# The order of a small product, two state loads and a norm broadcast in a one-core hybrid decoder step

## The chip, the cores and the metric

The kernel runs on one core of a Trainium2 chip. The metric is device microseconds (us) of one execution. An engine takes its instructions in the order in which they stand in its own queue: TensorE (PE, matrix products, with its weight loads shown apart as PEld), VectorE (DVE), ScalarE (ACT), GpSimd (POOL), and SyncE (SP), which here only issues transfers (DMA). Engines meet through semaphores, so an instruction that waits holds back all that stand behind it on its engine.

## What is computed

One layer of a hybrid decoder, for a prompt of 1024 tokens and for 8 sample sequences of 4 tokens (1056 columns in all, the last 32 being the samples). All data are float32; large products are made of three products of rounded halves, so that each counts three times on PE. Cut to what matters here:

```python
proj = rmsnorm(x, norm1) @ w_in                # -> z | x,B,C | dt | q | k | v
xbc  = silu(causal_conv4(x,B,C))
# state-space mixer, 8 heads in 2 groups, chunks of 128 tokens:
cb     = C_chunk @ B_chunk.T                   # one 128x128 product per chunk and group
y_diag = (cb * decay) @ (x * dt)
y_off  = C_chunk @ state * exp(acum)           # the state that came in
state  = state * chunk_decay + B_chunk.T @ (x * tail)
y = rmsnorm((y + x*d_skip) * silu(z))
# beside it windowed attention over q, k, v -> y_att
x  = x + concat(y, y_att) @ w_out
u  = causal_conv3(rmsnorm(x, norm2) @ w_up)
x  = x + (silu(gate) * val) @ w_down
```

For the sample sequences `state` is read from an input (8 states for each group of heads, 1 MB per group here), for the prompt it starts at zero.

## The kernel before

Activations lie with features on the 128 partitions and tokens along the columns. The program has these stretches, by the times of the profile: the input projection and the attention, to about 265 us; the state-space mixer with the projection for z, the last projections for x,B,C and the first output pieces between its steps, to about 390 us; the remaining output pieces, to 465 us; the up projection with its convolution, to 930 us (it is done in halves of 528 columns, tp = 0 and 1, and by a seven-product scheme on 2x2 blocks, whose block sums, `T1` to `T4` and the like, are made by VectorE); and the down projection, to the end.

The order is set in two steps. The string `PLAN` lists the steps of the mixer stretch: `u` a state unit (group, chunk; chunk 8 is the samples), `x` a projection with its convolution, `z` a gate block, `n` a gate norm, `a` and `s` the splitting of attention and mixer output into rounded halves, `o` an output piece (row block m, column quarter q). Then a list scheduler with a timeline of its own (`schedule_with_timeline_sim=True`) reorders the instructions of every engine, and so an edit in one function can move instructions of many others. Tiles come from pools with a fixed number of buffers; a tile of a full pool waits until the last reader of an older one is done.

What the change and the prediction touch:

- `ssd_unit(g, t, ...)` is one state unit. It transposes x (two blocks) and B into the PSUM tile `px` (L611), ACT copies them to `xt` (L614), POOL multiplies by dt and by the tail into `xw` and `xd` (L618, L619). The product of B and C, `pcb`, goes to the last 128 columns of the same `px` (L638), and VectorE masks it into `cb` (L640), which multiplies the decay `M` (tile `ab`, L646). Then come the products into `yy` (L653, L655) and the new state into `st` (L660).
- Its sample branch (t = 8) multiplies `xw` (L674), stores `bt` and `xd` to `smps` (L678, L679), and loads the 8 incoming states in four transfers of 256 KB into the two buffers of `h0` (L682), each followed by two products into `yy` (L685); `ys` (L687, L689) adds up, `yt` (L692) transposes back.
- The pool with the tag `y` has eight buffers; `fm` (the eight blocks of x, B and C), `yt` (attention output read back, L751) and `acc` (the residual read from `in_xT`, L774) take turns in them.
- `half_rstd(tp)` sums squares by products with ones (L852), takes the reciprocal root on VectorE (L134 to L140), transposes the six columns back to rows by PE (L859) and copies them (L861). `half_prep(tp)` calls it, scales the residual (L871) and makes the operands of the up projection (L883, L884, L888). It is called for tp = 0 between two output pieces of the first row block and for tp = 1 after the first up product (L1068).
- L147 is the inner product of all dense work (`dense`), L990 that of the up projection, L998 and L1012 add two of its products, L935 and L936 split its weights.

Of the kernel before, what the change touches and what calls it, by code (L numbers as in the profile page):

```python
# [46 lines left out]
def kernel(ctx, tc, xT, wxbc, wkv, wq, wz, wout, wup, wdn, cols, rows, cst, idm,  # L47
# [29 lines left out]
    def b3(ap, *shape):  # L77
        return ap.broadcast_to(list(shape))
# [519 lines left out]
    def ssd_unit(g, t, p, carry, te):  # L598
# [5 lines left out]
        hs = slice(4 * g, 4 * g + 4)  # L604
        px = psd.tile([128, 512], F32, tag="px", name="px", bufs=2)
        if smp:
            f4 = p.tile([128, 512], F32, tag="Cs", name="f4", bufs=2)[:, 0:384].rearrange("p (i c t) -> p i c t", i=3, c=4)
            for i, f in enumerate((x0, x1, Bm)):
                pool.tensor_copy(out=f4[:, i], in_=b3(f[:, tok].unsqueeze(1), 128, 4, NS))
        for i, f in enumerate((x0, x1, Bm)):  # L610
            pe.transpose(out=px[:, i * 128:(i + 1) * 128],  # L611
                         in_=f4[:, i].rearrange("p c t -> p (c t)") if smp else f[:, tok], identity=ident)
# [21 lines left out]
            act.activation(out=M[:, h], in_=M[:, h], func=AF.Relu, scale=-1.0,  # L634
                           bias=acum[:m, t, 4 * g + h:4 * g + h + 1])
        act.activation(out=M, in_=M, func=AF.Exp, scale=-1.0)
        pcb = px[:m, 384:384 + m]
        pe.matmul(out=pcb, lhsT=Bm[:, tok], rhs=Cm[:, tok], start=True, stop=True)  # L638
        cb = p.tile([128, 128], F32, tag="cb", name="cb")[:m, :m]
        dve.tensor_tensor(out=cb, in0=pcb, in1=(cs[:NS, K_TS:K_TS + NS] if smp else tri), op=ALU.mult)  # L640
        if smp:
# [33 lines left out]
                      rhs=xw[:m, 64 * h:64 * h + 64], start=True, stop=True)  # L675
        cm = p.tile([128, 8, NS], F32, tag="cm", name="cm", bufs=1)
        pool.tensor_tensor(out=cm, in0=b3(Cm[:, NP:T].unsqueeze(1), 128, 8, NS), in1=bmask, op=ALU.mult)
        sp.dma_start(out=smps[g, :, 0:128], in_=bt)  # L678
        sp.dma_start(out=smps[g, :, 128:384], in_=xd)  # L679
        for j in range(4):  # L680
            h0 = p.tile([128, 2, 256], F32, tag="h0", name="h0", bufs=2)
            sp.dma_start(out=h0, in_=h0T[:, g, 2 * j:2 * j + 2])  # L682
            for b in range(2):
                r = slice(32 * (2 * j % 4 + b), 32 * (2 * j % 4 + b) + 32)
                pe.matmul(out=yy[r, 256:512], lhsT=cm[:, 2 * j + b], rhs=h0[:, b], start=j < 2, stop=j >= 2)  # L685
        y = p.tile([128, 256], F32, tag="xd0", name="ys")
        dve.tensor_tensor(out=h4(y), in0=h4(yy[:, 256:512]),  # L687
                          in1=b3(te[:, 8 + 4 * g:12 + 4 * g].unsqueeze(2), 128, 4, 64), op=ALU.mult)
# [160 lines left out]
    def half_rstd(tp):  # L849
        ps = bank()  # L850
        for j in range(6):
            pe.matmul(out=ps[:88, j:j + 1], lhsT=ssum[tp][:, 88 * j:88 * j + 88], rhs=ones[:, 0:1], start=True, stop=True)  # L852
        v = pt_.tile([128, 2, 6], F32, tag="v2", name="v2")
        dve.tensor_scalar(out=v[:88, 0], in0=ps[:88, 0:6], scalar1=1.0 / D, scalar2=EPS, op0=ALU.mult, op1=ALU.add)
        rsqrt(pt_, v[:88, 1], v[:88, 0], 88, 6)
        for q in range(2):
            ps = bank()
            for j in range(3):
                pe.transpose(out=ps[:, 88 * j:88 * j + 88], in_=b3(v[:88, 1, 3 * q + j:3 * q + j + 1], 88, 128),  # L859
                             identity=ident[:88, :88])  # L860
            act.activation(out=ssum[tp][:, q * QC:q * QC + QC], in_=ps[:, :QC], func=AF.Copy)  # L861
        return ssum[tp]

    X2 = [{}, {}]

    def half_prep(tp):

        rb = half_rstd(tp)
        for m in (4, 5, 6, 7, 0, 1, 2, 3):
            h = half(m, tp)  # L870
            dve.scalar_tensor_tensor(out=h, in0=h, scalar=col(C_N2 + m), in1=rb, op0=ALU.mult, op1=ALU.mult)  # L871
# [73 lines left out]
    for i, m in enumerate((4, 5, 6, 7, 0, 1, 2, 3)):  # L945
        if i >= 4:
            w[m] = None
        for q in (2, 3):
            out_piece(m, q)
            if i == 0 and q == 2:  # L950
                half_prep(0)
        half_done(m, 1, i == 0)
    up_load(0)
    for j in range(7):
# [93 lines left out]
    for n, (cp, groups) in enumerate(SETS):  # L1048
        for g in groups:
# [15 lines left out]
                conv(cp, 0)  # L1065
            last = (n, *g), done
            if g == (0, 0):
                half_prep(1)  # L1068
    product(*last[0], 6)
    conv(last[0][1], 1)  # L1070
    sp.dma_start(out=fco, in_=fcot)
# [188 lines left out]
```

## Time and profile before

| | before |
|---|---|
| runs, us | 1192.59, 1192.26, 1187.1 |
| median, us | 1192.26 |
| the profiled execution, us | 1191.26 |
| its span, first to last instruction, us | 1189.5 |
| mean granted TensorE clock | 0.99 |
| PE busy | 1149.4 (97%) |
| VectorE busy | 906.0 (76%) |
| ScalarE busy | 513.0 (43%) |
| GpSimd busy | 134.8 (11%) |
| moved by DMA | 122.52 MB, mean 103 GB/s |

A row of the window table gives, for a stretch, its length and then the busy time and the number of instructions of PE, PEld, DVE, ACT and POOL, the granted clock of TensorE (1.00 is full speed), the busy share of the DMA engines and the rate. A row of the timeline gives start, length, engine, line, operation and tile, with "x4" where four like ones are merged, and in brackets how long the engine had been idle before and who released it. A row of the chain of waits gives start and length of a piece of the chain that ended last. The profiled execution is 1.76 us longer than its span.

### The profile page before, as it was taken

Reading aid. Unit: us, or ns where it says so; the run is one execution under the profiler, and the core shown is the slowest. Engines: PE = TensorE matmul, PEld = TensorE weight load, DVE = VectorE, ACT = ScalarE, POOL = GpSimd, SP = SyncE. Lnnn points to the kernel's source line nnn. Section 1 sums busy time; section 2 is a strip of 40 time slices with the busy share of each in tenths; the row PEclk is TensorE's granted clock in tenths of the full one; section 3 lists DMA queues with packets and bytes.
Section 4 is the critical chain, followed back from the end, with each engine's and each line's share of the span. In section 5 each row is a group of like instructions: output and inputs, shape, how many; then the busy total and the mean of one; then the engine's idle time right before and its main releaser. Section 6 shows DMA issues by size and latency. Waiting matters only on the chain.

```text
span 1189.5 us, 22050 instructions
## 1 busy us (share of the span) xinstructions
PE 1149.4 (97%) x8614; PEld 1106.5 (93%) x8614; DVE 906.0 (76%) x1886; ACT 513.0 (43%) x1048; POOL 134.8 (11%) x300
## 2 busy tenths in 40 slices
PE   8899989999979999899999999999999999999998
PEld 7899878888957999789999999999999999999998
DVE  7678868666888578998777777787777877677764
ACT  7435553446774334555455454545454421112110
POOL 0000001022253000011011010101010011001000
PEclk9999989998999999899999999999999999999999
DMA  8111102113465523122222222222222944224203
GB/s 295 63 60 62 33 19 75 48 50 111 131 221 160 173 73 131 36 81 98 74 72 90 73 90 73 90 73 81 81 71 75 380 149 160 97 91 133 92 9 147
DMA packets 52360, 122.52 MB, mean 103 GB/s; under 512 B 9232, under 2 KB 19984, under 8 KB 52240
## 3 DMA queue, kind: packets, MB, share of 16 engines
q1 hardware_dynamic: 52256, 121.12, 29.8%
q8 instruction: 67, 1.10, 0.4%
q14 instruction: 37, 0.30, 0.1%
HBM read 94.86 MB, written 27.26 MB: 103 GB/s over the span
## 4 chain that ended last, share of the span: by engine, by line
PE 89%; DVE 7%; DMA 2%; ACT 1%; issue 1%; SPq 0%; POOL 0%; DVEq 0%; ACTq 0%
PE ps L147 40%; PE ps L990 35%; PE ps L199 7%; PE sc L503 1%; PE ps L525 1%; DVE x2l L884 1%; DVE au L936 1%; DVE c L1032 1%; PE two L147 1%; DMA raw<-in_wup 1%; PE ps L517 1%; PE yy L653 1%; PE st L660 1%; PE ps L339 0%; PE px L611 0%
## 5 line engine op out<-in xcount | busy, mean ns | idle before, releaser
L990 PE MATMUL ps<-x2h,au 128*128 128x264 f32 x2464 | 456.1, 286 | 8.5 <-DVE au L936 2.8
L990 PEld LDWEIGHTS ps<-x2h,au 128*128 128x128 f32 x2464 | 385.0, 189 | 10.6 <-DVE au L936 3.5
L990 PE MATMUL ps<-x2l,au 128*128 128x264 f32 x1232 | 349.4, 285 | 0.1
L990 PEld LDWEIGHTS ps<-x2l,au 128*128 128x128 f32 x1232 | 232.8, 189 | 0.3 <-DVE x2l L884 0.3
L1105 DVE TENSOR_TENSOR acc<-acc,ps 128x352 f32<-128x352 f32 x264 | 131.5, 517 | 66.0 <-PE ps L147 65.5
L147 PE MATMUL ps<-xh,uh 128*128 128x264 f32 (+3 forms) x528 | 163.3, 315 | 8.9 <-ACT xh L182 5.9
L147 PE MATMUL ps<-gh,ul 128*128 128x352 f32 x528 | 170.1, 322 | 0.0
L147 PE MATMUL ps<-gl,uh 128*128 128x352 f32 x528 | 170.0, 322 | 0.0
L147 PE MATMUL ps<-gh,uh 128*128 128x352 f32 x528 | 167.8, 322 | 0.0
L147 PE MATMUL ps<-xh,ul 128*128 128x264 f32 (+3 forms) x528 | 163.7, 311 | 0.0
L147 PE MATMUL ps<-xl,uh 128*128 128x264 f32 (+3 forms) x528 | 163.3, 310 | 0.3 <-POOL xl L180 0.3
L116 ACT ACTIVATE uh<-raw 128x1024 fp32r<-128x1024 f32 (+3 forms) x59 | 55.9, 953 | 188.0 <-PE ps L147 166.9
L1032 DVE SCALAR_TENSOR_TENSOR c<-u,colt,c 128x1072 f32<-128x1072 f32 x88 | 116.7, 1329 | 3.6 <-ACT c L1030 3.6
L147 PEld LDWEIGHTS ps<-xh,uh 128*128 128x128 f32 x528 | 99.7, 190 | 13.7 <-ACT xh L182 6.3
L147 PEld LDWEIGHTS ps<-xl,uh 128*128 128x128 f32 x528 | 100.6, 191 | 1.8 <-POOL xl L180 0.9
L147 PEld LDWEIGHTS ps<-xh,ul 128*128 128x128 f32 x528 | 100.6, 190 | 1.0 <-issue 0.3
L936 DVE TENSOR_TENSOR au<-raw,au 128x512 fp32r<-128x512 f32 x115 | 78.8, 690 | 27.3 <-ACT au L935 27.3
L147 PEld LDWEIGHTS ps<-gl,uh 128*128 128x128 f32 x528 | 99.2, 188 | 0.4
L147 PEld LDWEIGHTS ps<-gh,ul 128*128 128x128 f32 x528 | 99.3, 188 | 0.0
L147 PEld LDWEIGHTS ps<-gh,uh 128*128 128x128 f32 x528 | 98.8, 188 | 0.0
L935 ACT ACTIVATE au<-raw 128x512 fp32r<-128x512 f32 x115 | 71.0, 625 | 60.7 <-DVE raw L923 31.5
L119 DVE TENSOR_TENSOR ul<-raw,uh 128x1024 fp32r<-128x1024 f32 (+3 forms) x55 | 60.5, 1105 | 7.0 <-ACT uh L116 6.9
(290 smaller groups left out, 1768.4 us busy)
## 6 DMA issues: line engine op xcount, KB each, us to landing
raw<-in_wup SPq DMA_DIRECT2D x46, 512.0 KB, 3.5
gr<-gd SPq DMA_DIRECT2D x22, 528.0 KB, 5.3
gd<-c SPq DMA_DIRECT2D x22, 512.0 KB, 2.6
raw<-in_wdn SPq DMA_DIRECT2D x22, 512.0 KB, 3.8
raw<-in_wout SPq DMA_DIRECT2D x12, 512.0 KB, 3.4
acc<-in_xT SPq DMA_DIRECT2D x16, 264.0 KB, 5.0
accd<-acc SPq DMA_DIRECT2D x16, 264.0 KB, 2.5
acc<-accd SPq DMA_DIRECT2D x8, 528.0 KB, 8.4
```

The lines of the kernel that those rows point to most:

```text
L116: act.activation(out=hi, in_=raw, func=AF.Copy)
L119: (e or dve).tensor_tensor(out=lo[:, i:i + n], in0=raw[:, i:i + n], in1=hi[:, i:i + n].bitcast(F32), op=ALU.subtract)
L147: pe.matmul(out=ps, lhsT=w(a, k), rhs=x(b, k), start=first and k == ks[0] and i == 0, stop=last and k == ks[-1] and i == 2)
L199: pe.matmul(out=ps[:m, :n], lhsT=x[k][c][:, a:a + m], rhs=w[k // nk][b][:, o:o + n], start=k == 0 and i == 0, stop=k == 7 and i == 2)
L503: pe.matmul(out=sb[:, v, c].rearrange("p i k -> p (i k)"), lhsT=qT[a][r, c], rhs=kT[b][r, o:o + 256], start=i == 0, stop=i == 2)
L517: pe.transpose(out=pt[:, h], in_=P[:, h], identity=ident)
L525: pe.matmul(out=po[64 * v:64 * v + 64, 0:256].rearrange("p (c q) -> p c q", c=2), lhsT=(vall[:, t - i] if i or not t else vdif[:, t - 1])[ ...
L935: act.activation(out=u[:, 0:512], in_=src, func=AF.Copy)
L936: dve.tensor_tensor(out=u[:, 512:1024], in0=src, in1=u[:, 0:512].bitcast(F32), op=ALU.subtract)
L990: pe.matmul(out=ps, lhsT=wgt[:, 512 * a + 128 * k:512 * a + 128 * k + 128], rhs=xx[b][:, k], start=opens and k == 0 and i == 0, stop=k == ...
L1032: dve.scalar_tensor_tensor(out=c[:, 0:n], in0=u[:, j:j + n], scalar=col(C_FW + 3 * m + j), in1=c[:, 0:n], op0=ALU.mult, op1=ALU.add)
L1105: dve.tensor_tensor(out=o, in0=o, in1=ps[:, :PC], op=ALU.add)
```

## The change

Three edits, each of code that is written in another place:

1. In every state unit the product `pcb` of B and C is issued ahead of the three transposes into the same `px`.
2. In the sample units the first two of the four loads of states are written at the unit's beginning; the two stores to `smps` now stand behind all four.
3. `half_prep(0)` is split: the norm sums and the reciprocal root (`half_rstd`) stay after output piece (4, 2), the broadcast and what follows (`half_bcast`) come after piece (4, 3).

```diff
@@ -604,9 +604,17 @@
         px = psd.tile([128, 512], F32, tag="px", name="px", bufs=2)
         if smp:
+
+            h0s = []
+            for j in range(2):
+                h0s.append(p.tile([128, 2, 256], F32, tag="h0", name="h0", bufs=2))
+                sp.dma_start(out=h0s[j], in_=h0T[:, g, 2 * j:2 * j + 2])
             f4 = p.tile([128, 512], F32, tag="Cs", name="f4", bufs=2)[:, 0:384].rearrange("p (i c t) -> p i c t", i=3, c=4)
             for i, f in enumerate((x0, x1, Bm)):
                 pool.tensor_copy(out=f4[:, i], in_=b3(f[:, tok].unsqueeze(1), 128, 4, NS))
+
+        pcb = px[:m, 384:384 + m]
+        pe.matmul(out=pcb, lhsT=Bm[:, tok], rhs=Cm[:, tok], start=True, stop=True)
         for i, f in enumerate((x0, x1, Bm)):
             pe.transpose(out=px[:, i * 128:(i + 1) * 128],
@@ -634,8 +642,6 @@
         act.activation(out=M, in_=M, func=AF.Exp, scale=-1.0)
-        pcb = px[:m, 384:384 + m]
-        pe.matmul(out=pcb, lhsT=Bm[:, tok], rhs=Cm[:, tok], start=True, stop=True)
         cb = p.tile([128, 128], F32, tag="cb", name="cb")[:m, :m]
@@ -675,14 +681,17 @@
-        sp.dma_start(out=smps[g, :, 0:128], in_=bt)
-        sp.dma_start(out=smps[g, :, 128:384], in_=xd)
         for j in range(4):
-            h0 = p.tile([128, 2, 256], F32, tag="h0", name="h0", bufs=2)
-            sp.dma_start(out=h0, in_=h0T[:, g, 2 * j:2 * j + 2])
+            if j < 2:
+                h0 = h0s[j]
+            else:
+                h0 = p.tile([128, 2, 256], F32, tag="h0", name="h0", bufs=2)
+                sp.dma_start(out=h0, in_=h0T[:, g, 2 * j:2 * j + 2])
             for b in range(2):
                 r = slice(32 * (2 * j % 4 + b), 32 * (2 * j % 4 + b) + 32)
                 pe.matmul(out=yy[r, 256:512], lhsT=cm[:, 2 * j + b], rhs=h0[:, b], start=j < 2, stop=j >= 2)
+        sp.dma_start(out=smps[g, :, 0:128], in_=bt)
+        sp.dma_start(out=smps[g, :, 128:384], in_=xd)
@@ -853,6 +862,9 @@
         rsqrt(pt_, v[:88, 1], v[:88, 0], 88, 6)
+        return v
+
+    def half_bcast(tp, v):
         for q in range(2):
             ps = bank()
@@ -863,9 +875,9 @@
-    def half_prep(tp):
-
-        rb = half_rstd(tp)
+    def half_prep(tp, v):
+
+        rb = half_bcast(tp, v)
@@ -948,7 +960,9 @@
             out_piece(m, q)
             if i == 0 and q == 2:
-                half_prep(0)
+                v0 = half_rstd(0)
+            elif i == 0:
+                half_prep(0, v0)
@@ -1065,7 +1079,7 @@
             if g == (0, 0):
-                half_prep(1)
+                half_prep(1, half_rstd(1))
```

What the scheduler made of it shows in the order of the built programs, at three places.

SP's queue around the sample unit of group 0 and after it. `h_3929` and `h_3933` are its first two loads before, `h_3937` and `h_3941` the second two, `h_4631` the first load of group 1; in the change the same are `h_3892`, `h_3894`, `h_3935`, `h_3939` and `h_4594`. Before:

```order
L631 DMA Cs<-ead 128x512
L678 DMA smps<-xt 128x128
L628 DMA ms<-acds 32x128
L679 DMA smps<-xd 128x256
L751 DMA yt<-yatt 128x2x384 x2
L115 DMA raw<-in_wout 128x1024
L628 DMA ab<-acd 128x512 x2
L631 DMA Cs<-ead 128x512
L774 DMA acc<-in_xT 128x528
L628 DMA ab<-acd 128x512
L682 DMA h_3937<-in_h0T 128x512
L682 DMA h_3941<-in_h0T 128x512
```

Now:

```order
L760 DMA yt<-yatt 128x2x384 x2
L636 DMA ms<-acds 32x128
L639 DMA Cs<-ead 128x512
L693 DMA smps<-xt 128x128
L694 DMA smps<-xd 128x256
L636 DMA ab<-acd 128x512 x2
L115 DMA raw<-in_wout 128x1024
L639 DMA Cs<-ead 128x512
L783 DMA acc<-in_xT 128x528 x2
L636 DMA ab<-acd 128x512
L689 DMA h_3935<-in_h0T 128x512
L689 DMA h_3939<-in_h0T 128x512
```

The attention output `yt` is now read ahead of the stores to `smps`, one more residual load stands ahead of the second pair of states, and the first pair stands where it stood: its two rows are far above these, the 62nd and 63rd of SP's queue before and now. The second pair of group 1 stood ahead of the reads of `yt` for the last column block and of eight residual loads; now it stands behind those reads and behind four of the eight loads.

PE at the second pair of states of group 0. Before:

```order
L638 MATMUL px<-fm 128x128 x2
L685 MATMUL yy<-h_3937,cm 32x256 x2
L611 MATMUL px<-idt,fm 128x128 x6
L685 MATMUL yy<-h_3941,cm 32x256 x2
L692 MATMUL yt<-idt,ys 128x128 x2
L660 MATMUL st<-xd,xt 128x256
L638 MATMUL px<-fm 128x128
```

Now:

```order
L147 MATMUL ps<-xh,ul 128x264
L692 MATMUL yy<-h_3935,cm 32x256 x2
L692 MATMUL yy<-h_3939,cm 32x256 x2
L617 MATMUL px<-fm 128x128
L619 MATMUL px<-idt,fm 128x128 x3
L617 MATMUL px<-fm 128x128
L619 MATMUL px<-idt,fm 128x128 x3
L701 MATMUL yt<-idt,ys 128x128 x2
```

The six transposes that stood between the two halves of the second pair are gone from there. Between the first pair and the second stand 17 dense products and two `pcb` before, and 18 dense products, one `pcb` and six transposes now.

VectorE at the preparation of the second half (tp = 1) for the up projection. Before:

```order
L936 TENSOR_TENSOR au<-raw,au 128x512 x2
L871 SCALAR_TENSOR_TENSOR acc<-acc,colt,ssum_5198 128x528 x8
L998 TENSOR_TENSOR u<-s_5934,ps 128x264
L998 TENSOR_TENSOR u<-s_5907,ps 128x264
L884 TENSOR_TENSOR x2l<-acc,x2h 128x528
L936 TENSOR_TENSOR au<-raw,au 128x512
L925 TENSOR_TENSOR t_6025<-raw 128x512
```

Now:

```order
L1012 TENSOR_TENSOR u<-s_5934,ps 128x264
L1012 TENSOR_TENSOR u<-s_5907,ps 128x264
L948 TENSOR_TENSOR au<-raw,au 128x512
L883 SCALAR_TENSOR_TENSOR acc<-acc,colt,ssum_5198 128x528 x8
L937 TENSOR_TENSOR t_6025<-raw 128x512
L896 TENSOR_TENSOR x2l<-acc,x2h 128x528 x5
```

The scaling of the second half stands three instructions later on VectorE. On PE its broadcast stands behind 134 products of the up projection before, and behind 156 now, and the first half's broadcast follows its norm sums by 47 dense products before and by 33 now; after that broadcast come 300 dense products before and 264 now. From the sample unit's first product to the last norm sum of the mixer PE has 153 dense products before and 219 now.

## The prediction

> **What bounds the kernel now.** I read the page's first lines, then the window table, the waits of PE between 255 and 396 us, the timelines of that stretch by engine, and the chain of waits around the norm of the second half.
>
> ```profile
> span 1189.5 us, 22050 instructions
> core 0: us, PE busy (x) PEld busy (x) DVE busy (x) ACT busy (x) POOL busy (x), PEclk, DMA share, GB/s
> 268.00:272.00 4.00, 1.64 (x11) 0.98 (x8) 4.00 (x10) 3.31 (x10) 2.33 (x3) 0.84 0.86 275
> 272.00:278.00 6.00, 6.00 (x19) 5.82 (x20) 4.43 (x9) 5.28 (x15) 1.02 (x2) 0.53 0.39 135
> 330.00:345.00 15.00, 10.44 (x75) 7.49 (x75) 10.45 (x20) 11.92 (x32) 10.48 (x15) 1.00 0.88 301
> 345.00:367.00 22.00, 17.36 (x168) 13.99 (x165) 20.23 (x60) 16.53 (x53) 5.73 (x11) 1.00 0.28 93
> 367.00:390.00 23.00, 21.36 (x167) 18.66 (x165) 18.81 (x63) 7.39 (x17) 10.82 (x14) 1.00 0.59 186
> 390.00:465.00 75.00, 75.00 (x621) 74.79 (x621) 52.97 (x104) 28.76 (x45) 0.40 (x4) 1.00 0.37 126
> 465.00:485.00 20.00, 20.00 (x171) 19.82 (x170) 16.12 (x39) 8.94 (x20) 1.62 (x4) 1.00 0.32 97
> 485.00:515.00 30.00, 24.32 (x163) 22.74 (x162) 28.61 (x50) 16.59 (x31) 0.68 (x4) 0.89 0.17 65
> 515.00:535.00 20.00, 18.22 (x148) 17.80 (x146) 19.66 (x29) 12.37 (x18) 4.10 (x8) 1.00 0.20 63
> 535.00:1189.50 654.50, 649.86 (x4832) 648.97 (x4832) 490.87 (x807) 240.56 (x395) 66.41 (x172) 1.00 0.30 105
> ```
>
> PE bounds all but a few places: from 390 to 485 it never rests, and after 535 it misses 4.6 of 654.5 us. The change takes no instruction away, so it can only win idle PE time. In the mixer stretch that is 4.56 us (330 to 345), 4.64 (to 367) and 1.64 (to 390), 10.8 us in all, and before it the start, where PE is busy for 1.64 of 4 us and then runs 6 us at a clock of 0.53. Elsewhere an edit can lose: in 485 to 535 VectorE is the full engine (28.61 of 30, 19.66 of 20 us) and PE waits for it.
>
> **The product ahead of its transposes.** At the start of the mixer:
>
> ```profile
> 269.64 0.49 PE L638 MATMUL px<-fm 128*128 128x128 f32 x2 [1.09 <-ACT xt L614]
> 271.93 1.22 PE L660 MATMUL st<-xd,xt 128*128 128x256 f32 x2 [0.97 <-POOL xd L619]
> 268.69 0.49 ACT L710 ACTIVATE ps<-gz 128x384 f32<-128x384 f32 x1 [4.48 <-DVE gz L709]
> 269.12 0.47 ACT L614 ACTIVATE xt<-px 128x384 f32<-128x384 f32 x1
> 269.67 1.64 POOL L618 TENSOR_TENSOR xd<-xt,dt 128x256 f32<-128x256 f32 x1 [2.62 <-ACT xt L614]
> 271.27 0.61 POOL L619 TENSOR_TENSOR xd<-xt,tailw 128x256 f32<-128x256 f32 x1
> ```
>
> `pcb` writes the tile that ACT is reading, and so waited 1.09 us for the copy `xt`. Ahead of the transposes it does not. But the next instruction, `st`, waited for POOL until 271.93, and that chain stays: ACT's copy stands behind the gate's L710, which waits for VectorE, then POOL needs 1.64 and 0.61. The wait changes its name, and the dense products behind `st` begin at the same time. Value 0. Bounds: if POOL came earlier by the 1.09, a gain of 1.1; if the now unbroken idle time from about 268.9 to 271.9 prolonged the slow stretch by half of its price (half of (1 - 0.53) x 6.00 = 2.8), a loss of 1.4. From 278 to 330 the units run between dense products; there is nothing to win.
>
> The earlier `pcb` also ends the use of B earlier, and the buffer goes to `yt`:
>
> ```profile
> 327.08 0.88 SPq L751 DMA_DIRECT2D yt<-yatt  x2
> 333.68 3.97 DVE L180 TENSOR_TENSOR xl<-fm,xh 128x384 fp32r<-128x384 f32 x4 [2.41 <-ACT xh L179]
> 268.08 1.40 SPq L682 DMA_DIRECT2D h<-in_h0T  x2
> 334.36 0.90 SPq L682 DMA_DIRECT2D h<-in_h0T  x2
> 339.68 0.63 PE L685 MATMUL yy<-h,cm 128*32 128x256 f32 x4 [2.38 <-DMA h<-in_h0T]
> 340.23 0.88 PE L611 MATMUL px<-idt,fm 128*128 128x128 f32 x6
> 341.04 0.63 PE L685 MATMUL yy<-h,cm 128*32 128x256 f32 x4
> 339.72 0.47 DVE L640 TENSOR_TENSOR cb<-px,cs 128x128 f32<-128x128 f32 x2
> ```
>
> In the new order `yt` stands ahead of the stores, and ACT's splitting, for which VectorE waited 2.41 us, can begin earlier. That alone does not move PE, which then waits for the states.
>
> **The states.** The first pair was issued at 268.08, some 65 us ahead of its products, and stands at the same place now: that part of the edit does nothing. The wait of 2.38 us is for the second pair, issued at 334.36, when the first pair's buffers come free; the edit leaves that as it is. What moves is beside it: between the pairs PE has about four small matmuls more (0.81 us for six, from 340.23 to 341.04, so 0.5 us of cover), and the six transposes between the halves of the second pair are gone, so that `ys` can begin 0.8 us earlier; two `cb` (0.47) now stand between the parts of `ys` on VectorE, which is the full engine from there to 367. One residual load more stands ahead in the queue. Together -1.3 + 0.4 = -0.9, and with `yt` out of the way of the loads I take -1.3. Bounds: 2.38 + 0.8 + the 0.3 that remains of cover = -3.5; if the additional 264 KB at 301 GB/s (0.9 us) land ahead of the states and VectorE sets the end, +1.0.
>
> Group 1's second pair is the part that speaks against the change:
>
> ```profile
> 372.47 0.82 SPq L682 DMA_DIRECT2D h<-in_h0T  x2
> 378.90 3.76 SPq L774 DMA_DIRECT2D acc<-in_xT  x8
> DMA to landing us min/median/max: 3.9/7.0/7.0
> 366.13 1.13 DVE L740 SCALAR_TENSOR_TENSOR fm<-fm,colt,nb 128x384 f32<-128x384 f32 x2
> 378.36 1.49 DVE L180 TENSOR_TENSOR xl<-fm,xh 128x288 fp32r<-128x288 f32 x2 [1.44 <-ACT xh L179]
> 421.49 0.86 PE ps L852 x12
> 422.35 5.83 PE ps L147 x47
> 428.64 36.64 PE ps L147 x300
> 465.28 5.82 PE ps L990 x48
> 473.44 9.39 PE ps L990 x74
> 483.90 3.17 DVE acc L871 x5
> 489.42 0.68 DVE u L998 x2
> L936 DVE TENSOR_TENSOR au<-raw,au 128x512 fp32r<-128x512 f32 x115 | 78.8, 690 | 27.3 <-ACT au L935 27.3
> ```
>
> Before, it was issued at 372.47 and PE did not wait. Now four residual loads stand ahead: 3.76 / 8 = 0.47 us each to issue, 1.9 in all, then 3.9 to 7.0 to land, so 5.8 to 8.9 us. PE's cover between the pairs is 5 + 31 = 36 dense products at 5.83 / 47 = 0.124, or 4.5, and 0.6 for small ones: 5.1. The stall is 0.7 to 3.8, or nothing if the loads go before the buffers come free. I take +1.5, near the low end, since the transfers now stand in a queue that asks for `yt` earlier.
>
> The 66 dense products more in this stretch (219 against 153) are 8.2 us of PE work, but 52 stand ahead of the second sample unit, where PE was idle for 1.64 us in all. I take -1.0 (-1.6 to 0) for that.
>
> **The norm.** Between the first half's sums (421.49) and its broadcast PE did 47 dense products without a pause: there is nothing to win. The new order puts that broadcast 36 products (4.5 us) closer to the up products; VectorE, busy for 52.97 of 75 us until 465, has room. The second half's broadcast stands behind 156 up products in place of 48 + 12 + 74 = 134: 22 at 9.39 / 74 = 0.127, or 2.7 us later, and the scaling (483.90) with it, at the start of the stretch that VectorE fills. VectorE does three instructions more before it, two of 0.34 and one of 0.69: 1.4 us that it need not do after. Value +2.7 - 1.4 = +1.3. Bounds 0 (if the sums wait for VectorE anyway) and +2.7.
>
> **The sum:** 0 - 1.3 + 1.5 - 1.0 + 1.3 = +0.5 us. The profiled execution took 1191.26, which is 1.0 under the median shown, so **1191.8 us**. The bounds add up to -6.2 and +8.9; not all fall on one side, and the forecast's own range is 1187 to 1197.
>
> By the Trainium skill (TensorE: Matmul & The Clock Gate, Part 1), the clock falls to half after an idle window of about 3.4 us and comes back after about 3.4 us of sustained work. The clock of 0.53 after the start and 1.00 around the stall of 2.38 us agree with that in kind, though the start's slow stretch is nearer to 6 us. By it, any stall that this change brings is worth only itself while it stays under 3.4 us; the slow rival below would be 1.7 us of slow clock dearer than its stall, where the row gives 2.8.
>
> **Rivals.**
>
> *Faster: the mixer stretch was held by VectorE and the transfers, and the 66 products fill it.* If the stretch keeps its length while 8.2 us of PE work move into it, the idle 10.8 us shrink by as much, and 1.3 come back in the norm: 1191.26 - 8.2 + 1.3 = 1184.4. For it: VectorE is busy for 20.23 of 22 us in 345 to 367. Against it: in just that window the new order has the same 36 dense products as the old, and the products added stand where PE had little idle time. 0.21.
>
> *Slower: the second pair of group 1 waits behind a residual load whose buffer is not free.* A residual load needs the buffer of a split block. If it waits for the last block, the path is L740 (1.1), ACT's part (about 0.8) and L180 (1.5), 3.4 us after the norm's broadcast, then two issues (0.9) and 7.0 to land: 11.3, against PE's cover from there, 47 dense products (5.8) and 1.1 of small ones. The stall is 4.4, long enough to bring a slow stretch such as that of 272 to 278 (2.8): 7.2 us. The gain of 1.0 is gone, the other terms cancel: 1191.26 + 7.2 = 1198.5. It decides from a stall of about 3.5 us. For it: the queue's order, and the 3.76 us that the eight loads took. Against it: of those eight, issued at 0.47 us each, hardly one waited. 0.14.
>
> *The change does not do what it says.* The scheduler had loaded the states early and put products between sums and broadcast already, and the `pcb` wait was one of several. Then all that is left is a reshuffled order that costs as much as it gains: 1191.3. 0.20.
>
> **How the numbers follow.** The forecast itself has 0.45. It and the third rival are no change within 0.5% (6 us, about what a measurement of this kernel can tell from no change): 0.65. Faster 0.21, slower 0.14. The range 1183.5 to 1199 takes in both other cases' times and leaves out a sum in which nearly all bounds fall on one side.
>
> **What would show it.** Right: no PE wait for `xt` in front of `pcb`, but one at the first `st` until about 272; a wait for the second pair of group 0 of 1 to 2 us; one for group 1's of 0.7 to 2.5; the second half's scaling 2 to 3 us later after the first up product. The forecast is wrong if PE's idle time from 330 to 390 falls below 5 us, or if the wait for group 1's states passes 3.5 us with a clock under 1.00 behind it.

## The result

| | runs | median, us | ratio to before, 95% interval |
|---|---|---|---|
| before | 5 | 1191.3 (1187.1 to 1192.59) | |
| changed | 5 | 1210.58 (1204.56 to 1212.15) | 1.0153 (1.013 to 1.0175) |

The change makes the kernel 1.5% slower. The forecast of 1191.8 us, its range (1183.5 to 1199) and its likeliest cases were wrong.

### The profile page after: what moved, and what is told of

Read it like the earlier page. It is cut to its first block, busy times and chain, and to the rows that moved or that the text cites. A ratio compares the mean times of both kernels' runs of the same rounds, so it can differ in the third digit from the quotient of the medians.

```text
span 1210.3 us, 22105 instructions
## 1 busy us (share of the span) xinstructions
PE 1159.8 (96%) x8614; PEld 1113.0 (92%) x8614; DVE 917.5 (76%) x1886; ACT 517.4 (43%) x1048; POOL 143.0 (12%) x300
## 4 chain that ended last, share of the span: by engine, by line
PE 87%; DVE 6%; DMA 3%; ACT 2%; issue 1%; POOL 0%; SPq 0%; DVEq 0%; ACTq 0%; POOLq 0%
PE ps L147 38%; PE ps L1004 34%; PE ps L199 6%; PE sc L503 1%; PE ps L525 1%; DMA raw<-in_wup 1%; DVE x2l L896 1%; DVE au L948 1%; PE yy L659 1%; PE ps L517 1%; PE two L147 1%; DMA h<-in_h0T 1%; PE st L666 0%; DMA xr<-in_xT 0%; PE px L619 0%
## 5 line engine op out<-in xcount | busy, mean ns | idle before, releaser
L147 PE MATMUL ps<-xh,uh 128*128 128x264 f32 (+3 forms) x528 | 166.6, 321 | 15.9 <-ACT xh L182 5.8
L147 PE MATMUL ps<-gh,ul 128*128 128x352 f32 x528 | 170.1, 322 | 0.0
L147 PE MATMUL ps<-gl,uh 128*128 128x352 f32 x528 | 170.0, 322 | 0.0
L147 PE MATMUL ps<-gh,uh 128*128 128x352 f32 x528 | 167.9, 322 | 0.6 <-ACT gh L179 0.6
L147 PE MATMUL ps<-xl,uh 128*128 128x264 f32 (+3 forms) x528 | 166.5, 316 | 1.4 <-DVE xl L180 1.1
L147 PE MATMUL ps<-xh,ul 128*128 128x264 f32 (+3 forms) x528 | 165.3, 314 | 0.0
L147 PEld LDWEIGHTS ps<-xh,uh 128*128 128x128 f32 x528 | 102.8, 196 | 20.9 <-ACT xh L182 6.3
L147 PEld LDWEIGHTS ps<-xl,uh 128*128 128x128 f32 x528 | 103.4, 196 | 3.9 <-DVE xl L180 1.9
L147 PEld LDWEIGHTS ps<-xh,ul 128*128 128x128 f32 x528 | 102.9, 195 | 1.0 <-issue 0.2
L147 PEld LDWEIGHTS ps<-gh,uh 128*128 128x128 f32 x528 | 98.8, 188 | 0.9 <-ACT gh L179 0.9
L147 PEld LDWEIGHTS ps<-gl,uh 128*128 128x128 f32 x528 | 99.2, 188 | 0.4
L147 PEld LDWEIGHTS ps<-gh,ul 128*128 128x128 f32 x528 | 99.3, 188 | 0.0
```

The lines of the kernel that those rows point to most:

```text
L147: pe.matmul(out=ps, lhsT=w(a, k), rhs=x(b, k), start=first and k == ks[0] and i == 0, stop=last and k == ks[-1] and i == 2)
```

## The profile after

The profiled execution took 1212.15 us. Its length and the window table, in the stages of the prediction, with 390 to 465 split in three:

```profile
span 1210.3 us, 22105 instructions
268.00:272.00 4.00, 1.17 (x7) 0.99 (x6) 4.00 (x10) 4.00 (x13) 3.31 (x4) 1.00 0.88 269
272.00:278.00 6.00, 6.00 (x32) 6.00 (x31) 4.06 (x7) 5.22 (x14) 0.37 (x2) 0.72 0.24 92
330.00:345.00 15.00, 9.99 (x63) 7.32 (x63) 8.95 (x14) 9.20 (x24) 7.46 (x9) 0.85 0.74 213
345.00:367.00 22.00, 18.65 (x148) 14.88 (x146) 18.61 (x53) 14.53 (x48) 8.10 (x13) 0.87 0.33 107
367.00:390.00 23.00, 17.09 (x109) 14.25 (x109) 15.31 (x35) 6.35 (x17) 10.91 (x15) 0.85 0.38 114
390.00:410.00 20.00, 16.15 (x128) 14.76 (x129) 13.61 (x42) 7.84 (x12) 0.00 (x0) 0.97 0.60 200
410.00:418.00 8.00, 8.00 (x46) 8.00 (x47) 3.06 (x12) 0.26 (x1) 0.00 (x0) 0.65 0.34 124
418.00:465.00 47.00, 47.00 (x393) 46.79 (x393) 27.04 (x56) 13.24 (x22) 0.00 (x0) 1.00 0.30 104
```

The row of each stage gives its length, the busy time and count of PE, PEld, DVE, ACT and POOL, the granted clock and the DMA's share and rate. One number makes the stages comparable: PE's loss, the length of a stage less its busy time multiplied by the granted clock. For 367 to 390 that is 23 - 17.09 x 0.85 = 8.5 us now, and it was 23 - 21.36 = 1.6.

| stage, us | loss before | loss after | difference | term in the prediction |
|---|---|---|---|---|
| 268 to 278 | 5.4 | 4.5 | -0.9 | 0 |
| 330 to 367 | 9.2 | 12.3 | +3.1 | -1.3 |
| 367 to 390 | 1.6 | 8.5 | +6.9 | +1.5 - 1.0 |
| 390 to 465 | 0 | 7.1 | +7.1 | 0 |
| first 95 us of the up projection (from 465.3, from 481.9) | 10.4 | 13.2 | +2.8 | +1.3 |
| sum | 26.6 | 45.6 | +19.0 | +0.5 |

The stages of more than one row, and the last, are summed from their windows (the last from windows of 20, 30, 20 and 25 us). The sum accounts for 19.0 of the 20.8 us between the two spans. About half is idle time (PE idle 40.1 us before, 50.5 now), the other half work at a slow clock (PE busy 1149.4, now 1159.8).

Where PE waited, by its timeline:

```profile
270.95 0.70 PE L666 MATMUL st<-xd,xt 128*128 128x256 f32 x2 [2.83 <-POOL xd L627]
340.10 1.28 PE L692 MATMUL yy<-h,cm 128*32 128x256 f32 x6 [3.69 <-DMA h<-in_h0T]
379.10 0.59 PE L147 MATMUL ps<-xh,uh 128*128 128x264 f32 x1 [4.37 <-DVE acc L787]
395.14 0.64 PE L692 MATMUL yy<-h,cm 128*32 128x256 f32 x8
397.52 0.64 PE L147 MATMUL ps<-xh,uh 128*128 128x264 f32 x3 [1.26 <-ACT xh L179]
409.78 0.59 PE L147 MATMUL ps<-xh,uh 128*128 128x264 f32 x1 [2.54 <-ACT uh L116]
```

The second pair of states of group 0 came late by 3.69 us (2.38 before). At 379.10 a new wait of 4.37 us stands for `acc`, an output piece's addition on VectorE that frees a PSUM bank. At 409.78 PE waited for output weights, in a stretch where it had never rested before. VectorE and GpSimd ahead of the longest wait:

```profile
371.70 0.98 DVE L134 TENSOR_SCALAR rs<-yms 128x3 int32<-128x3 int32 x1
372.59 0.15 DVE L136 TENSOR_SCALAR rs<-yms 128x3 f32<-128x3 f32 x1
373.61 1.53 DVE L135 TENSOR_SCALAR rs<-rs 128x3 int32<-128x3 int32 x1
375.38 1.22 DVE L139 TENSOR_TENSOR rs<-rs 128x3 f32<-128x3 f32 x1
376.63 1.39 DVE L140 SCALAR_TENSOR_TENSOR rs<-rs 128x3 f32<-128x3 f32 x1
378.06 0.65 DVE L138 TENSOR_TENSOR rs<-rs 128x3 f32<-128x3 f32 x1
378.63 0.42 DVE L787 TENSOR_TENSOR acc<-acc,ps 128x264 f32<-128x264 f32 x1
...
370.36 2.29 POOL L180 TENSOR_TENSOR xl<-yt,xh 128x384 fp32r<-128x384 f32 x2 [2.90 <-ACT xh L179]
374.12 0.99 POOL L180 TENSOR_TENSOR xl<-yt,xh 128x384 fp32r<-128x384 f32 x1
375.31 1.68 POOL L649 TENSOR_TENSOR ab<-ms,cb 32x128 f32<-32x128 f32 x4 [0.19 <-DVE cb L646]
376.95 2.48 POOL L180 TENSOR_TENSOR xl<-yt,xh 128x384 fp32r<-128x384 f32 x3
```

Most operations on three columns (`rs`, the gate norm's reciprocal root) take 0.15 to 0.17 us. Here they take up to 1.53 while GpSimd works beside them, and `acc` stands behind seven of them. The five longest took 5.77 us where five calm ones take about 0.8, and that difference is enough for the wait of 4.37 us. Before, three of them took about 0.94 each in the same place, but three of the additions stood ahead of these:

```profile
370.81 0.43 DVE L778 TENSOR_TENSOR acc<-acc,ps 128x264 f32<-128x264 f32 x1
371.22 0.76 DVE L778 TENSOR_TENSOR acc<-acc,ps 128x264 f32<-128x264 f32 x2
372.29 0.94 DVE L138 TENSOR_TENSOR rs<-rs 128x3 f32<-128x3 f32 x1
373.26 0.94 DVE L139 TENSOR_TENSOR rs<-rs 128x3 f32<-128x3 f32 x1
374.24 0.93 DVE L140 SCALAR_TENSOR_TENSOR yms<-rs 128x3 f32<-128x3 f32 x1
371.23 3.93 POOL L180 TENSOR_TENSOR xl<-yt,xh 128x384 fp32r<-128x384 f32 x4 [0.85 <-ACT xh L179]
```

SyncE's queue for the same stretch:

```profile
333.50 0.86 SPq L689 DMA_DIRECT2D h<-in_h0T  x2
379.46 9.01 SPq L783 DMA_DIRECT2D acc<-in_xT  x4
389.99 0.80 SPq L689 DMA_DIRECT2D h<-in_h0T  x2
402.20 1.57 SPq L115 DMA_DIRECT2D raw<-in_wout  x2
408.23 3.11 SPq L115 DMA_DIRECT2D raw<-in_wout  x2
```

Issuing four residual loads took 9.01 us (eight took 3.76 before); most likely they waited for buffers. Group 1's second pair was issued at 389.99 (372.47 before). PE did not wait for it: it arrived there only at 395.14.

## The experiments

Each ratio is to the kernel before on the same chip. Of the built programs one more number is used: how many dense products (L147) stand on PE between the first product with a loaded state and the last gate norm's sums. It is 152 before and 215 in the changed kernel (the 153 and 219 of the prediction, and the 153 of the expectations, count from the sample unit's first product into `yy`). I call an order with about 150 of them short and one with about 215 long. Two orders of the same count can differ elsewhere.

### The edits apart (e1, e2)

e1 is the first edit alone:

```diff
+        pcb = px[:m, 384:384 + m]
+        pe.matmul(out=pcb, lhsT=Bm[:, tok], rhs=Cm[:, tok], start=True, stop=True)
         for i, f in enumerate((x0, x1, Bm)):
...
-        pcb = px[:m, 384:384 + m]
-        pe.matmul(out=pcb, lhsT=Bm[:, tok], rhs=Cm[:, tok], start=True, stop=True)
```

> Only the first edit: the product of B and C ahead of the transposes. Theory A (this edit is what lengthens the mixer: its new order puts the splitting of the attention output on GpSimd beside the small reciprocal-root operations on VectorE, with an output piece's addition behind them, and PE idles 4.4 us and then runs slowly): 1203 to 1209 us, and a PE wait of about 4 us for acc shortly after 370 us. Theory B (the norm's later broadcast costs it): within 2 us of the kernel before, 1189 to 1194, and no such wait. Theory C (the two edits harm each other, each alone is harmless): the same as B.

e2 is the third alone:

```diff
-                half_prep(0)
+                v0 = half_rstd(0)
+            elif i == 0:
+                half_prep(0, v0)
```

> Only the third edit: an output piece between the first half's norm sums and its broadcast. Theory A: 1189 to 1195 us, with the stretch up to 390 us as in the kernel before. Theory B: 1204 to 1211, with the loss after 420 us. Theory C: 1189 to 1195, and then the edits together must cost more than the sum of the two alone.

Measured: e1 1212.82 us, 1.0172 (1.0139 to 1.0206), in the long order; e2 1192.26, 1.0009 (0.9989 to 1.003), in the short one. Theory A holds, with a time above the range given for it: the first edit costs all of it. The second does nothing: with it or without it, the built program has the same order on every engine. In e1 the wait for `acc` is there, and one that the changed kernel does not have:

```profile
376.56 0.59 PE L147 MATMUL ps<-xh,uh 128*128 128x264 f32 x1 [4.36 <-DVE acc L779]
446.88 0.67 PE L860 MATMUL ps<-idt,v 88*128 88x88 f32 x6 [2.94 <-DVE v L140]
```

So the third edit did what it says, but only in the long order, where e1's norm sums have too little behind them. The two times (1.0172 and 1.0153) do not tell it apart.

### The stretched reciprocal root (e3, e4)

The scratch of the gate norms' reciprocal root moves to free columns of the norm's PSUM bank, and the two products of a Newton step change places, so that no operation has two operands in SBUF (`t`, `h` and the integer scratch are now in PSUM, `y` stays in SBUF):

```diff
-            e.tensor_tensor(out=t, in0=y, in1=y, op=ALU.mult)
-            e.tensor_tensor(out=t, in0=t, in1=h, op=ALU.mult)
+            e.tensor_tensor(out=t, in0=y, in1=h, op=ALU.mult)
+            e.tensor_tensor(out=t, in0=t, in1=y, op=ALU.mult)
```

> The changed kernel, with the scratch values of the gate norms' reciprocal root in PSUM in place of SBUF, so that none of those small VectorE operations reads two operands in SBUF; as many operations as ever, the same work on GpSimd. Theory A with its cause in the memory side (a VectorE operation with two SBUF operands waits while GpSimd works in SBUF): the small operations beside GpSimd's splitting take 0.15 to 0.25 us in place of 0.5 to 1.5, the PE wait of 4.37 us and the slow stretch behind it (2.9 us) go, 1202 to 1206 us. Rival (those operations were late for another reason, such as waits between their semaphores, or the stall only moves to the next thing that is late): the small operations keep 0.5 us or more, or the time stays within 3 us of 1210.6.

> The kernel before, with the same scratch values in PSUM. In its profile the stretched operations (0.94 us each, three of them at 372 to 375 us) held up nothing that PE needed, so by theory A it is worth 0 to 2 us: 1189 to 1192. If the memory side also held PE up elsewhere in the mixer, 1184 to 1188.

Measured: e3 1204.04 us, 1.0108 (1.0073 to 1.0143); e4 1192.25, 1.0011 (0.9992 to 1.003). VectorE and GpSimd in e3's timeline, and then one row of its window table:

```profile
372.13 0.16 DVE L139 TENSOR_TENSOR nb<-rs,nb 128x3 f32<-128x3 f32 x1
372.87 0.16 DVE L140 TENSOR_TENSOR nb<-nb,rs 128x3 f32<-128x3 f32 x1
373.07 0.16 DVE L141 SCALAR_TENSOR_TENSOR rs<-nb,rs 128x3 f32<-128x3 f32 x1
...
372.30 2.53 POOL L181 TENSOR_TENSOR xl<-yt,xh 128x384 fp32r<-128x384 f32 x3
```

```profile
367.00:390.00 23.00, 21.39 (x150) 18.34 (x151) 13.75 (x50) 5.12 (x12) 9.38 (x13) 0.93 0.50 157
```

The small operations take 0.16 us beside the same splitting on GpSimd, and the wait for `acc` is gone. The loss in 367 to 390 falls from 8.5 to 3.1, by 5.4; the median falls by 6.5, and the ratio by 0.45%, with intervals that just overlap. So operands in SBUF, beside GpSimd's work there, are what stretches the operations. Whether it takes two is not settled: the integer operations L134 and L135 read one tensor, were stretched in the changed kernel, and have their scratch in PSUM here as well. Nor is all of the 5.4 us shown to be the stretching's, because the scheduler made another order for e3 (114 dense products ahead of group 1's first loaded states, 106 in the changed kernel), in which an addition stands ahead of the Newton steps:

```profile
371.78 0.43 DVE L790 TENSOR_TENSOR acc<-acc,ps 128x264 f32<-128x264 f32 x1 [0.33 <-PE ps L148]
```

The Trainium skill (SBUF — State Buffer, "SBUF: two separate sides") says that VectorE and GpSimd share one port pair as an exclusive lock, which an operation with two SBUF inputs needs against a GpSimd operation that reads SBUF; for operations on two tensors this run agrees (0.16 us here, up to 1.39 in the changed kernel). In the short order (e4) the same stretch held up nothing that PE needed.

### The states, the stores and the residual's queue (e5 to e10)

e5 and e7 give the loaded states four buffers, in the changed kernel and in the kernel before; e10 three, in the changed one:

```diff
-            h0 = p.tile([128, 2, 256], F32, tag="h0", name="h0", bufs=2)
+            h0 = p.tile([128, 2, 256], F32, tag="h0", name="h0", bufs=4)
```

> The changed kernel with four buffers for the incoming states in place of two, so that all four loads of a group can be issued as early as the first two. If the longer wait for the second pair (3.69 us, 2.38 before) and the slow clock from 340 to 349 us cost what they show: 1204 to 1208 us, no PE wait for the states. If the stretch from 330 to 367 us is held by VectorE anyway (the kernel with the third edit alone ran at a clock of 0.72 and 0.88 there and lost nothing by it): 1209 to 1211 us.

> The kernel before with four buffers for the incoming states. Its wait for the second pair is 2.38 us at full clock. If PE's wait is what sets the end of that stretch: 1187.5 to 1189.5 us. If VectorE holds the stretch: 1190 to 1192 us.

> The changed kernel with three buffers for the incoming states: the order stays as it is, but one load of group 0's second pair is issued as early as the first pair, and one of group 1's ahead of the residual loads. Only the last load of each group stays where it was. If the place in the queue of the last load sets the time: the wait of 3.69 us falls to 2.5 to 3.5, 1207 to 1211 us. If the bytes that are in flight at the same time set it: the wait falls by half, 1204 to 1208 us.

e6 (the stores) and e9 (the residual loads) take transfers out of SyncE's queue, in the changed kernel; e8 has the mends of e3, e5 and e6 at once:

```diff
-        sp.dma_start(out=accd[m][:, tp * HT:tp * HT + HT], in_=h)
+        pool.dma_start(out=accd[m][:, tp * HT:tp * HT + HT], in_=h)
...
-            sp.dma_start(out=half(m, tp), in_=xT[m][:, tp * HT:tp * HT + HT])
+            pool.dma_start(out=half(m, tp), in_=xT[m][:, tp * HT:tp * HT + HT])
```

> The changed kernel with the stores of the finished residual rows issued from GpSimd's queue in place of SyncE's, so that a load of output weights no longer stands behind a store that waits for its additions. If PE's wait of 2.54 us for those weights at 409.78 us and the slow clock behind it (410 to 465: 55 us of work at a mean clock of 0.95, 2.75 us) come from that place in the queue: no such wait, 1204 to 1207 us. If the weights are late because their buffers come free late: 1209 to 1212 us, the wait stays.

> The changed kernel with the three mends at once: scratch in PSUM, four buffers for the states, stores from GpSimd's queue. If each of the three waits costs what it shows and they add: 6.6 (measured) + 2 to 6 + 3 to 6 off 1210.6, so 1192 to 1199 us. If the scheduler's order of the mixer itself is the slower one and the waits only move: 1200 to 1204 us, no better than the scratch alone.

> The changed kernel with the loads of the residual (acc from in_xT) issued from GpSimd's queue in place of SyncE's; the order of the other work is the same but for a few rows. If the states of group 1 and the output weights come late because they stand behind residual loads that wait for buffers (the four that took 9.01 us from 379.46), then the second pair is issued by about 380 us, its products stand 8 to 10 us earlier than 395.21, the waits at 397 (1.26) and 409.78 (2.54) and the slow clock behind them go, and the group-0 wait of 3.69 us falls to 2 to 3: 1201 to 1206 us, with the 4.37 us for acc still there. If those waits come from elsewhere: 1209 to 1213 us.

| run | order | median, us | ratio, 95% interval |
|---|---|---|---|
| e5 | short (150) | 1193.58 | 1.0036 (1.0009 to 1.0063) |
| e7 | short (150) | 1190.85 | 1.0005 (0.9986 to 1.0024) |
| e8 | short (150) | 1197.85 | 1.0073 (1.0052 to 1.0094) |
| e6 | long (215) | 1207.53 | 1.0173 (1.0139 to 1.0206) |
| e9 | long (215) | 1207.04 | 1.0149 (1.0122 to 1.0177) |
| e10 | long (215) | 1204.20 | 1.0127 (1.0102 to 1.0152) |

e5 gave far more than the wait of 3.69 us could be worth, and e7 shows that the buffers themselves are worth nothing. What e5 had done was to bring a short order back. e8 has the same count: its time lies in the range for waits that add, but in an order that is not the changed kernel's, so it does not show that they add. At 1.0073 it shows that a short order, too, can lose as much as e14 to e16 do below. e9 is the clean test, since its order differs from the changed kernel's in a few rows only: PE no longer waits for group 0's states, yet nothing measurable is won. In e10, whose order is the changed kernel's, that wait fell from 3.69 to 2.20 us and the time lies in the range given for the bytes in flight, but the two ratios' intervals overlap. These rows are of PE and of SyncE's queue in e9:

```profile
371.80 0.59 PE L147 MATMUL ps<-xh,uh 128*128 128x264 f32 x1 [4.36 <-DVE acc L787]
381.45 1.71 SPq L689 DMA_DIRECT2D h<-in_h0T  x2
```

Group 1's second pair is late here too (381.45), with no residual load ahead of it in the queue: it waits for its buffers, and so for PE's own order (PE's products with the first pair begin at 379.08 in e9, at 387.63 in the changed kernel and at 371.81 before). My expectation that the residual loads hold it was wrong, and so was that of e6: the wait for the weights stayed (2.87 us) with the stores out of the queue. The weights' loads there began when the conversion of the last ones had freed their buffers, and that conversion waited for PE.

### PE kept busy in a wait (e11)

```diff
         rb = half_rstd(tp)
+        if tp == 1:
+            psx = bank()
+            for k in range(4):
+                pe.matmul(out=psx[:, :264], lhsT=ident, rhs=rb[:, :264], start=True, stop=True)
```

> The kernel before with four additional products (128x264, float32, their result is not used) that read the broadcast root mean square of the second half, so that PE has work while it waits 2.38 us for x2h at 488.86 us. If an idle wait of 2.4 us is enough to bring the slow clock that follows there (0.56 in the next 3 us, a mean of 0.89 from 485 to 515): the clock stays near 1.00 there and the time is 2 to 4 us shorter, 1186.5 to 1188.5. If the clock falls for another reason, or VectorE sets the end of that stretch anyway: 1190 to 1193 us.

Measured: 1192.98 us, 1.0022 (1.0008 to 1.0036). Inconclusive: the clock from 485 to 515 rose to 0.99 from 0.89, but the four products took 3.50 us, and the scheduler moved the broadcast ahead of its inputs, where PE now waits:

```profile
481.02 0.67 PE L859 MATMUL ps<-idt,v 88*128 88x88 f32 x6 [3.63 <-DVE v L140]
```

### The order or the place of the product (e12 to e14)

The product stands ahead of the transposes only in the units that a condition names, and where it stood in the others: `smp and g == 1` (e12), `g == 0` (e13), `not smp` (e14).

> The product of B and C ahead of the transposes in one single unit, the sample unit of group 1; all other units as in the kernel before. The scheduler's order then has 114 dense products ahead of group 1's first state products and 215 ahead of the last gate norm's sums (the kernel before 72 and 153, the changed one 106 and 215). Theory O (the loss comes with the order: dense products are spent ahead of the mixer's last chain, and then there are none to cover it): 1200 to 1210 us. Theory P (the loss comes from where the product stands in the units): 1190 to 1193 us.

> The product of B and C ahead of the transposes in the nine units of group 0 alone. The order then has 72 dense products ahead of group 1's first state products and 153 ahead of the last norm's sums, as in the kernel before. Theory O: 1188 to 1194 us. Theory P: half of the loss, about 1200 us.

> The product of B and C ahead of the transposes in all 16 units of the prompt, not in the two sample units. The order has 97 and 168 dense products at the two places, between the other orders. Theory O: between them, 1193 to 1200 us. Theory P: 16 of 18 units, 1206 to 1211 us.

Measured: one unit moved, long order: 1205.07 us, 1.0149 (1.0109 to 1.0189). Nine units moved, short order: 1193.29, 1.0045 (1.0016 to 1.0073). Sixteen, an order between (168): 1196.52, 1.0071 (1.0055 to 1.0087). Theory P, the place of the product, is out: one unit of 18 costs as much as all. e13 is in the range of theory O, but its interval leaves out 1.0, so about 0.45% are lost there that the count does not explain. In e12 VectorE, GpSimd and PE show the stretched operation once more, in its plainest form:

```profile
365.22 3.52 DVE L135 TENSOR_SCALAR rs<-rs 128x3 int32<-128x3 int32 x1
366.77 3.43 POOL L180 TENSOR_TENSOR xl<-yt,xh 128x384 fp32r<-128x384 f32 x4
370.92 0.59 PE L147 MATMUL ps<-xh,uh 128*128 128x264 f32 x1 [4.38 <-DVE acc L782]
```

### An edit that has nothing to do with the change (e15 to e18)

Two, three or three smaller products whose result is not used, in the kernel before, after the copy `xt` of the first unit; e17 is the changed kernel with the mends of e3 and e9.

```diff
+        if g == 0 and t == 0:
+            for k in range(2):
+                pe.matmul(out=px[:, 0:256], lhsT=xt[:, 0:128], rhs=xt[:, 0:256], start=True, stop=True)
```

> The kernel before, unchanged but for two additional products (128x256, float32) at the mixer's first unit, after the copy xt, whose result is not used; the product of B and C stands where it stood. The scheduler answers with an order that has 96 dense products ahead of group 1's first states and 216 ahead of the last norm's sums. Theory O (the order costs the time, whatever edit brings it): 1199 to 1209 us, with a PE wait of about 4.4 us for an output piece's addition. Theory P: 1188 to 1192 us. Beside that, if PE's idle time at the mixer's start is what halves its clock, the clock from 272 to 278 us is 0.9 or more in place of 0.53.

> The same with three such products; this order has 97 and 168 dense products at the two places, as the kernel with the edit in the 16 prompt units, which took 1196.5 us. Theory O: 1193 to 1198 us, and no wait of 4.4 us. Theory P: 1188 to 1192.

> The changed kernel with two of the mends: the reciprocal root's scratch in PSUM and the residual loads from GpSimd's queue. Its order has 114 dense products ahead of group 1's first states and 189 ahead of the last norm's sums. If the wait for the states and the stretched operations are separate parts of the loss: 1197 to 1202 us. If the first mend had already taken what can be had in this order: 1203 to 1206 us.

> The kernel before with three additional products of 128x128 at the mixer's first unit, after the copy xt, whose result is not used. Here the scheduler keeps the order of the kernel before exactly, these three products apart. Theory O: no loss, and if keeping PE busy at the mixer's start keeps its clock (0.53 from 272 to 278 us before, half of 6 us), a gain of up to 2.8 us: 1187.5 to 1191 us. If such products themselves cost what e15 and e16 lost: 1196 to 1200 us.

| run | order | median, us | ratio, 95% interval |
|---|---|---|---|
| e15 | long (216) | 1198.57 | 1.0064 (1.0044 to 1.0084) |
| e16 | between (168) | 1199.25 | 1.0056 (1.0031 to 1.0082) |
| e17 | between (189) | 1201.00 | 1.0083 (1.0058 to 1.0109) |
| e18 | short (152) | 1190.29 | 0.9992 (0.997 to 1.0014) |

e18 has the order of the kernel before, those three products apart, and costs nothing; e15 and e16 cost 0.6%. An unrelated edit that brings a longer order loses too. But the order's count is not the whole price: e15 was expected to have the wait for `acc` and does not, and it lost less than half of what the changed kernel lost; e16 came out just above its range. In e15 six of the small operations are stretched as well (0.72 to 1.02 us), but no addition stands behind them. Its clock from 272 to 278 us is 1.00, as expected. What it has is the wait for the weights, in PE's timeline:

```profile
397.43 0.39 PE L147 MATMUL ps<-xh,uh 128*128 128x264 f32 x1 [3.20 <-ACT uh L116]
```

e17, in an order between the two, came to 1201.0, in the range given for separate parts; since its order moved as well, it does not settle how the parts add.

No version beat the kernel before: e2, e4, e7 and e18 are level with it.

## Why the prediction was wrong

**The step that failed** is the value of "-1.0 (-1.6 to 0)" for the 66 dense products that the order moves into the mixer stretch, and behind it the sentence that PE "never rests" from 390 to 485, taken as a place with nothing to lose. I priced these products by the idle time that they could fill. They are not filling: they stand in PE's queue ahead of group 1's sample unit and of the last norms, make that chain later, and are missing behind it. Measured in place of -1.0: +7.1 in 390 to 465, and +6.9 in 367 to 390, of which the term in the next paragraph is the larger part. e15 moves as many products and has no wait for `acc`; its 0.64% are 7.6 us. e12, e15 and e18 show that the loss comes with the scheduler's order and not with the edit's place. That these products are what costs within the order is not shown by itself, since no run moves them alone and the short orders of e8 and e13 lose as well. That the wait for the weights at 409.78 comes from the missing products is read from the traces (every long order has it, at 2.4 to 3.2 us, and so have e16 and e17 of those between, e14 at 0.7; e6 shows that it isn't the stores) and was not tried by itself.

**A term that was not in the sum** is the wait of 4.37 us and the slow clock behind it. The rows for it stood in the trace of before: three operations at 0.94 us each at 372 to 375, beside GpSimd's splitting. I read VectorE's order for what stands behind what, with durations from calm rows. e3 puts this part at up to 5.4 us in its stage. e15 shows that stretched operations cost PE nothing when no addition stands behind them, so the order decides here as well.

**The product ahead of its transposes** (0): right at its place. PE waits for `st` until 270.95, as foreseen, and the stage is 0.9 better. But it was priced as if an edit's cost lay where the edit is; all of the loss comes with this edit, 100 us later.

**The states of group 0** (-1.3, a wait of 1 to 2 us): wrong in sign, a wait of 3.69 us and a slow clock, +3.1 with the stage behind it. In the total it matters little: e9 has no such wait and is not measurably faster, and e18, level with the kernel before, lost 11.7 us in the same stage.

**Group 1's second pair** (+1.5, a wait of 0.7 to 3.8): the pair was issued 17.5 us later, behind residual loads that took 9.01 us. But e9 has it late without them, since the first pair's products free its buffers, and those came 15.8 us later. The price was wrong, since PE itself came later still: no wait. The slower rival was right in its sign and named this place; its mechanism did not decide, and that its stall of 4.4 us is so near the 4.37 measured for `acc` is chance.

**The norm** (+1.3, the scaling 2 to 3 us later): the scaling comes 24.4 us after the first up product (506.11 less 481.70), and 18.6 before, so 5.8 later (the 22 products at 0.127 are 2.8 us, not 2.7). The stretch lost 2.8 more, just over the bound of 2.7. e2 loses nothing there, so this too belongs to the first edit's order.

**The clock**: I let any stall under 3.4 us cost only itself. The wait of 2.54 us was followed by 8 us at 0.65, a further 2.8. The trace of before had the sign of it: I named its stall of 2.38 us at 339.68, with the clock at 1.00, and passed over an equal one, behind which the clock was 0.56 for 3 us (0.89 in the row from 485 to 515):

```profile
488.86 0.53 PE L990 MATMUL ps<-x2h,au 128*128 128x264 f32 x2 [2.38 <-ACT x2h L883]
```

**"The change does not do what it says"**, at 0.20, was right for the second edit. Its "reshuffled order that costs as much as it gains" is the error of the whole forecast in one phrase: the order was taken to be neutral. Neither of the stated signs of failure came: PE's idle time from 330 to 390 did not fall below 5 us but rose to 14.3 (10.8 before), and the waits that passed 3.5 us with a slow clock behind them were for group 0's states and for `acc`, not for group 1's states. I had looked for the miss in the wrong places.

## What to carry to other kernels

Where a scheduler sets the order, price the order and not the edit: count what stands ahead of the longest chain on each engine before and after, and treat work moved ahead of that chain as cover taken from what follows it. The count alone does not give the price: look also at which small operations now stand ahead of what the busy engine waits for. Work moved into a stretch is not free, even where that stretch has idle time, if the stretch it leaves has none. Test a surprising time with an unrelated edit that brings a like order, and with one that leaves the order alone.

## What the hardware showed that I had not expected

**Small VectorE operations wait out GpSimd's.** An operation on three columns took 0.15 us alone and up to 3.52 us beside GpSimd operations on SBUF (e12); with one operand in PSUM it stayed at 0.16 (e3). L136, which reads one float32 operand and stands between the stretched ones, never took more than 0.17 in the changed kernel, while the integer operations L134 and L135, which also read one, were stretched; why they differ is open.

**The clock falls after waits well under 3.4 us.** In the profiles of all twenty kernels, from 265 to 600 us, 40 waits of PE were 2.4 us or longer, and in the 3 us behind 36 of them the mean clock was 0.50 to 0.75; the exceptions are waits of 2.42, 2.47 and 2.50 us (1.00) and one of 2.75 (0.90). Of 30 waits from 2.0 to 2.4 us, 27 were followed by 0.50 to 0.87. In these traces every slow stretch of that part runs at 0.50 and lasts 3.41, 6.83 or 10.24 us, so that one costs 1.7 us of work or more (an estimate, half of 3.41). The Trainium skill (TensorE: Matmul & The Clock Gate, Part 1) puts the idle window at about 3.4 us; here the measurement decides: 2.4 us, with the thin work that stood around these waits, were mostly enough. The mixer's start shows that one long wait isn't needed. Before, PE's longest wait there is 1.09 us, but PE was busy for only 1.64 of the 4 us from 268. In e18 the longest wait is the same, and the additional products make it 2.83 of 4:

```profile
268.26 0.94 PE L617 MATMUL px<-xt 128*128 128x128 f32 x6 [1.09 <-ACT xt L614]
```

The clock from 272 to 278 is then 1.00 where it was 0.53:

```profile
268.00:272.00 4.00, 2.83 (x18) 2.59 (x19) 4.00 (x9) 4.00 (x13) 3.35 (x4) 1.00 1.04 258
272.00:278.00 6.00, 6.00 (x38) 5.90 (x37) 4.94 (x10) 5.56 (x15) 1.64 (x3) 1.00 0.19 71
```

The time did not follow: the loss from 268 to 278 fell from 5.4 to 1.2 us, and 330 to 367 lost 11.7 in place of 9.2: PE waits there for the states (2.17 us) and for VectorE in e18 too, and its clock was 0.78 from 330 to 345, where it had been 1.00.
